# Gate and up of the second and third FFN chunk as products of scaled float16 pairs

## The chip, the cores and the metric

The kernel runs on one NeuronCore of a Trainium2 chip. The metric is the device time of one execution in microseconds (us). Besides TensorE (PE, its weight loads are listed apart as PEld) the core has VectorE (DVE), ScalarE (ACT), GpSimd (POOL) and SyncE (SP, which here only issues DMAs); each works through its own queue in order, and semaphores tie them together.

## What is computed

One step of a hybrid diffusion backbone with one layer: 128 context tokens and 1024 latent tokens, model width 1024, all in float32. Attention and a bidirectional mLSTM stand side by side behind one input projection and are merged by one output projection; the SwiGLU feed-forward network (FFN) follows. The part that matters here is its first product:

```python
def swiglu(h, w_gu, w_down):
    g, u = jnp.split(h @ w_gu, 2, axis=-1)
    return (jax.nn.silu(g) * u) @ w_down

h2 = rmsnorm(x, norm2_w) * (1 + sc2) + sh2          # sc2, sh2 from the conditioning vector
x = x + g2 * swiglu(h2, w_gu, w_down)
```

`w_gu` is 1024 x 5632 (gate and up, 2816 columns each), `w_down` 2816 x 1024. The result is wanted at about float32 accuracy. A single pass of TensorE does not hold that many bits, so the kernel splits each operand into a high and a low part and adds three products: high by high, high by low, low by high.

## The kernel before

The 1152 tokens are nine blocks of 128 (block 0 is the context), and for the FFN three chunks of three blocks (`CB = 3`, `CT = 384` tokens, `NCH = 3`). The program runs in stages: modulation and norm of the input; input projection of the keys, values and gates; four mLSTM heads, each projected while the scan of the head before is worked on beside it (`weave`, `beside`); the query projection; then, for each chunk, attention, output projection and FFN. Attention of chunk c+1 is woven into the FFN of chunk c, so from chunk 0 on TensorE always has FFN products beside the attention.

The order inside a stage is written out with Python generators: `weave(main, side, ...)` takes a step of `side` every so many units of `main`. A scheduler then orders each engine's queue by a simulated timeline of its own (`schedule_with_timeline_sim`), with some parts marked more urgent (`hot`). So a change of one instruction may shift the order of others behind it.

Weights come in pieces of 128 x 1024 float32 (512 KB). `load_piece` (L139) handles one: SP issues the DMA into a `raw` tile (two buffers), ACT casts it to the high part `whi` (L152, five buffers), and DVE (each third piece) or POOL (the others) subtracts to get the low part `wlo` (L135, five buffers). A `raw` buffer is free for the next DMA when the subtraction is done; `whi` and `wlo` are free when TensorE has used them. High and low parts are `float32r`: 4 bytes, which TensorE takes in one pass.

`norm2` (L1141) makes the FFN's input for one block: ACT scales by the row's inverse RMS, TensorE transposes, DVE (or ACT) applies the modulation, ACT casts to the high part and DVE or POOL subtracts. The two tiles `aTh` and `aTl` (`a_tiles`, L970) lie in the buffers `b2` and `b3` and serve all three chunks one after the other. `gate_up` (L1193) goes over 22 column blocks f of 128; for each it loads a gate piece and an up piece and calls `products` (L1187), 8 x 3 matmuls of 128 x 128 by 384 columns each, into one PSUM bank. The first two f of chunk 0 go through `gate_up_pair` with 256 tokens first and 128 later. Behind each f, ACT takes tanh(g/2) from PSUM, DVE forms (tanh + 1) * u * g in two operations (L1217, L1218), and ACT and POOL split the result into `hl`, high and low. After a group of four or five f, `down` (L1225) multiplies with `w_down` in matmuls of 512 columns, in two halves of the output width, and `add_gated` adds to the residual through a temporary `t2` (three buffers).

At the end of chunk c the last `down` is woven with `norm2` of chunk c+1 (L1354). A step that the change copies stands in `k_work` (L575): a scale that is a power of two, taken from the maximum of the values by a transposition on TensorE, five small DVE operations and a matmul that spreads it over the partitions.

The functions that the change touches, with their lines:

Of the kernel before, what the change touches and what calls it, by code (L numbers as in the profile page):

```python
# [2 lines left out]

# [5 lines left out]
F32 = mybir.dt.float32  # L9
# [36 lines left out]
def hybrid_step(ctx: ExitStack, tc: tile.TileContext, I: dict, O: dict):  # L46
# [71 lines left out]

    def rsqrt(tp, ss, n, inv, cap=24, plus=EPS):

        v = tp.tile([P, cap], F32, name=nm("rv"), tag="rv", bufs=2)[:, :n]
        y = tp.tile([P, cap], F32, name=nm("ry"), tag="ry", bufs=2)[:, :n]
        t = tp.tile([P, cap], F32, name=nm("rt"), tag="rt", bufs=2)[:, :n]
        h = tp.tile([P, cap], I32, name=nm("rh"), tag="rh", bufs=2)[:, :n]
        dve.tensor_scalar(out=v, in0=ss, scalar1=inv, scalar2=plus, op0=ALU.mult, op1=ALU.add)
        dve.tensor_scalar(out=h, in0=v.bitcast(I32), scalar1=1, scalar2=None, op0=ALU.logical_shift_right)
        dve.tensor_scalar(out=y.bitcast(I32), in0=h, scalar1=-1, scalar2=0x5F3759DF, op0=ALU.mult, op1=ALU.add)
        for _ in range(3):
            dve.tensor_tensor(out=t, in0=y, in1=y, op=ALU.mult)
            dve.scalar_tensor_tensor(out=t, in0=t, scalar=-0.5, in1=v, op0=ALU.mult, op1=ALU.mult)  # L130
            dve.scalar_tensor_tensor(out=y, in0=t, scalar=1.5, in1=y, op0=ALU.add, op1=ALU.mult)
        return y
# [5 lines left out]

    def load_piece(srcs, shape, dve_every=3, raw=None, own=None):  # L139

        a, b = shape
        n = a * b

        def view(t):
            return t[:, :n].rearrange("p (a b) -> p a b", b=b)

        raw = raw or wp.tile([P, 1024], F32, name=nm("raw"), tag="raw", bufs=2)
        hi = own[0] if own else wp.tile([P, 1024], F32R, name=nm("whi"), tag="whi", bufs=5)
        lo = own[1] if own else wp.tile([P, 1024], F32R, name=nm("wlo"), tag="wlo", bufs=5)
        for part, ap_ in srcs:  # L150
            dma(part(view(raw)), ap_)
        nc.scalar.copy(hi[:, :n], raw[:, :n])  # L152
# [11 lines left out]
    sil = cp.tile([P, KD, 2], F32, name="sil")  # L164
    bcol = cp.tile([P, 48], F32, name="bcol")
    ncol = cp.tile([P, 16], F32, name="ncol")
    vsc = cp.tile([P, 4], F32, name="vsc")

    es_a = ExitStack()
# [375 lines left out]
    def norm_rope(qp, cc, ss, x, nb, nh, w, rb):  # L545
# [5 lines left out]
        act(sq, xf, AF.Square)  # L551
        ssum = qp.tile([P, 20], F32, name=nm("nrs"), tag="nrs", bufs=2)[:, :n]
        dve.tensor_reduce(out=ssum, in_=sq, axis=AX.X, op=ALU.add)
# [20 lines left out]

    def k_work(qp, cc, ss, kw):  # L575
        norm_rope(qp, cc, ss, kall[:, 9:10], 1, NKV, kw, (0, 0))
# [5 lines left out]
        dma(O["new_cache_v"][0, 0], vall[:, 9])  # L582
        qone = qp.tile([1, P], F32, name="qone")
        dve.memset(qone, 1.0)

# [194 lines left out]
    def beside(*sides):  # L780

        due = [0.0] * len(sides)
        while True:
# [5 lines left out]
            yield  # L789

    es_r = ExitStack()
    ada = ada_rest(es_r.enter_context(tc.tile_pool(name="adp", bufs=1, side="right", reuse_waits="tile")))
# [33 lines left out]

    cc, ss = tables(kw)
    kwork = k_work(qp, cc, ss, kw)
# [3 lines left out]
    emit(kwork)  # L832
    scan = head_mlstm(3, sts[3])
    cc, ss = tables(qw)
# [132 lines left out]
    ft = ctx.enter_context(tc.tile_pool(name="ft", bufs=1, side="right", reuse_waits="tile"))  # L967
    fp = ctx.enter_context(tc.tile_pool(name="fp", bufs=1, side="right", reuse_waits="tile"))

    def a_tiles():  # L970
# [170 lines left out]
    def norm2(c, a, i):  # L1141

        x1 = a["x1"][i]
        if "h2" not in a:
            a["h2"] = a_tiles()
        th, tl = a["h2"]
# [3 lines left out]
        for half in range(2):  # L1150
            with hot(800):
                y = fp.tile([P, 512], F32, name=nm("y"), tag="y", bufs=2)
                act(y, x1[:, half * 512 : (half + 1) * 512], AF.Copy, scale=r)
                ps = bank()
                for j in range(4):
                    transpose(ps[:, j * P : (j + 1) * P], y[:, j * P : (j + 1) * P])
                full = both[:, half * 4 : half * 4 + 4]
                for j in range(4):
                    k = half * 4 + j
                    if j == 0 and c == 0:  # L1160
                        act(full[:, j, :], ps[:, j * P : (j + 1) * P], AF.Identity, scale=scale2[:, k, cnd : cnd + 1], bias=shift2[:, k, cnd : cnd + 1])
                        continue
                    dve.tensor_scalar(  # L1163
                        out=full[:, j, :], in0=ps[:, j * P : (j + 1) * P],
                        scalar1=scale2[:, k, cnd : cnd + 1], scalar2=shift2[:, k, cnd : cnd + 1],
                        op0=ALU.mult, op1=ALU.add)
                oh = th[:, half * 4 : half * 4 + 4, i * P : (i + 1) * P]
                nc.scalar.copy(oh, full)
                sub(tl[:, half * 4 : half * 4 + 4, i * P : (i + 1) * P], full, oh.bitcast(F32), "pool" if c == 0 else "dve")
            yield True  # L1170

    def gate_up_pair(a, fs):

        a["early"] = []
        for f in fs:
# [3 lines left out]
            for j, off in enumerate((0, D_FF)):  # L1179
                src = w_gu[:, off + f * P : off + (f + 1) * P].rearrange("(k p) n -> p k n", p=P)  # L1180
                wh, wl = load_piece([(full_view, src)], (KD, P))
                ws.append((wh, wl))
# [10 lines left out]
    def gate_up(a, f0, nf):  # L1193
# [3 lines left out]
        for f in range(f0, f0 + nf):  # L1197
# [8 lines left out]
            else:  # L1206
                pg, pu = bank(), bank()
                for off, ps in ((0, pg), (D_FF, pu)):
                    src = w_gu[:, off + f * P : off + (f + 1) * P].rearrange("(k p) n -> p k n", p=P)
                    wh, wl = load_piece([(full_view, src)], (KD, P))  # L1210
                    products(ps[:, 0:CT], wh, wl, th, tl)
# [3 lines left out]
            for cs, g, u in parts:  # L1215
                act(tn[:, cs], g, AF.Tanh, scale=0.5)
                dve.scalar_tensor_tensor(out=tn[:, cs], in0=tn[:, cs], scalar=1.0, in1=u, op0=ALU.add, op1=ALU.mult)  # L1217
                dve.tensor_tensor(out=tn[:, cs], in0=tn[:, cs], in1=g, op=ALU.mult)  # L1218
            hl = hlp.tile([P, 2, CT], F32R, name=nm("hl"), tag="hl", bufs=5)
# [70 lines left out]

    cur, nxt = {}, {}
    cur["x1"], nxt["x1"] = new_x1(0), new_x1(1)
# [49 lines left out]
    for c in range(NCH):  # L1342
        if c + 1 < NCH:
# [16 lines left out]
            cur = nxt  # L1360
            nxt = cur["next"] = {}
        else:
# [59 lines left out]
```

## Time and profile before

| what | value |
|---|---|
| runs shown | 1618.33, 1618.56, 1621.84 us; median 1618.56 |
| the profiled execution: its time, its span | 1619.03 us, 1617.1 us |
| mean granted TensorE clock in it | 0.977 |
| PE, DVE, ACT, POOL busy | 1532.5, 965.3, 689.8, 618.0 us |
| first product of the FFN, end of its last | about 623 us, about 1600 us |

A matmul's listed duration is its latency; the matmuls are pipelined, and one starts long before the one ahead of it ends. The cost of a matmul in a dense stream is the distance between two starts (called pitch here), which the timeline shows. Groups list busy time, the mean of one instruction in ns, and the idle time of the engine ahead of them with what ended it. A row of stretches gives, after the bounds and the length, the busy time and the number of instructions of PE, PEld, DVE, ACT and POOL, then the granted clock, the DMA engines' busy share and GB/s.

### The profile page before, as it was taken

Reading aid. Unit: us, or ns where it says so; the run is one execution under the profiler, and the core shown is the slowest. Engines: PE = TensorE matmul, PEld = TensorE weight load, DVE = VectorE, ACT = ScalarE, POOL = GpSimd, SP = SyncE. Lnnn points to the kernel's source line nnn. Section 1 sums busy time; section 2 is a strip of 40 time slices with the busy share of each in tenths; the row PEclk is TensorE's granted clock in tenths of the full one; section 3 lists DMA queues with packets and bytes.
Section 4 is the critical chain, followed back from the end, with each engine's and each line's share of the span. In section 5 each row is a group of like instructions: output and inputs, shape, how many; then the busy total and the mean of one; then the engine's idle time right before and its main releaser. Section 6 shows DMA issues by size and latency. Waiting matters only on the chain. (4 is left out here: it accounts for less than half of the span.)

```text
span 1617.1 us, 23358 instructions
## 1 busy us (share of the span) xinstructions
PE 1532.5 (95%) x8670; PEld 1366.1 (84%) x8670; DVE 965.3 (60%) x1969; ACT 689.8 (43%) x1193; POOL 618.0 (38%) x392
## 2 busy tenths in 40 slices
PE   6899999899898968999999999999999999999996
PEld 2888888898676757998989899898898989999995
DVE  4842363957877668577663646767674474432445
ACT  3522242424534556555643344565552453333322
POOL 1511030413345324443445344444344445544443
PEclk8999999999898988999999999999999999999998
DMA  9244443303155865777773446777684445534441
GB/s 358 67 155 125 117 142 52 82 22 71 50 183 134 180 153 116 174 181 178 180 179 113 148 153 216 188 179 175 156 185 131 131 144 176 151 127 146 144 130 65
DMA packets 386311, 232.71 MB, mean 144 GB/s; under 512 B 169910, under 2 KB 346502, under 8 KB 386198
## 3 DMA queue, kind: packets, MB, share of 16 engines
q1 hardware_dynamic: 384342, 228.04, 52.5%
q10 hardware_dynamic: 1856, 3.19, 0.6%
q8 instruction: 68, 1.11, 0.3%
q14 instruction: 45, 0.37, 0.1%
HBM read 181.16 MB, written 11.69 MB: 119 GB/s over the span
## 5 line engine op out<-in xcount | busy, mean ns | idle before, releaser
L135 POOL TENSOR_TENSOR wlo<-raw,whi 128x1024 fp32r<-128x1024 f32 (+1 forms) x159 | 390.2, 2459 | 512.3 <-ACT whi L152 474.4
L152 ACT CAST whi<-raw 128x1024 fp32r<-128x1024 f32 x239 | 245.0, 1026 | 361.7 <-DMA raw<-in_w_gu_dram 112.8
L1190 PE MATMUL mm<-aTl,whi 128*128 128x384 f32 (+2 forms) x1088 | 363.6, 334 | 0.0
L1189 PE MATMUL mm<-aTh,whi 128*128 128x384 f32 (+2 forms) x1088 | 362.5, 335 | 0.8 <-DVE tn L1217 0.8
L1191 PE MATMUL mm<-aTh,wlo 128*128 128x384 f32 (+2 forms) x1088 | 363.2, 334 | 0.0
L1189 PEld LDWEIGHTS mm<-aTh,whi 128*128 128x128 f32 x1088 | 204.5, 188 | 2.2 <-DVE tn L1217 1.4
L1190 PEld LDWEIGHTS mm<-aTl,whi 128*128 128x128 f32 x1088 | 204.9, 188 | 0.7
L1191 PEld LDWEIGHTS mm<-aTh,wlo 128*128 128x128 f32 x1088 | 204.9, 188 | 0.2
L135 DVE TENSOR_TENSOR wlo<-raw,whi 128x1024 fp32r<-128x1024 f32 (+1 forms) x80 | 98.4, 1230 | 151.7 <-ACT whi L152 147.8
L1008 PE MATMUL mm<-whi,hl 128*128 128x512 f32 x372 | 146.4, 398 | 0.8 <-ACT hl L1221 0.7
L1009 PE MATMUL mm<-wlo,hl 128*128 128x512 f32 x372 | 146.9, 396 | 0.0
L1010 PE MATMUL mm<-whi,hl 128*128 128x512 f32 x372 | 144.3, 396 | 0.8 <-POOL hl L135 0.8
L399 PE MATMUL wi<-whi,hTh 128*128 128x384 f32 (+2 forms) x392 | 135.9, 347 | 5.2 <-ACT hTh L341 5.1
L925 DVE SCALAR_TENSOR_TENSOR pl<-pr,st,ph 128x1152 f16<-128x1152 f32 (+1 forms) x72 | 111.6, 1550 | 47.7 <-ACT ph L924 47.6
L401 PE MATMUL wi<-whi,hTl 128*128 128x384 f32 (+2 forms) x392 | 133.6, 343 | 1.3 <-POOL hTl L135 1.3
L400 PE MATMUL wi<-wlo,hTh 128*128 128x384 f32 (+2 forms) x392 | 133.5, 341 | 0.0
L921 ACT ACTIVATE pr<-S,st 128x1152 f32<-128x1152 f32 (+1 forms) x72 | 81.2, 1128 | 99.7 <-DVE st L920 90.6
L135 POOL TENSOR_TENSOR hl<-tn,hl 128x384 fp32r<-128x384 f32 x66 | 83.5, 1266 | 105.0 <-ACT hl L1221 104.9
L998 DVE TENSOR_TENSOR x<-x,t 128x512 f32<-128x512 f32 x102 | 116.9, 1168 | 0.8
L1217 DVE SCALAR_TENSOR_TENSOR tn<-tn,mm 128x384 f32<-128x384 f32 (+2 forms) x68 | 36.6, 539 | 134.2 <-PE mm L1191 100.4
L918 PE MATMUL S<-kst,qT 128*128 128x384 f32 (+1 forms) x400 | 88.1, 356 | 13.9 <-ACT pr L921 13.8
L920 DVE TENSOR_REDUCE st<-S 128x1 f32<-128x1152 f32 (+1 forms) x72 | 88.8, 1233 | 20.7 <-PE S L918 20.3
(323 smaller groups left out, 2714.2 us busy)
## 6 DMA issues: line engine op xcount, KB each, us to landing
raw<-in_w_gu_dram SPq DMA_DIRECT2D x132, 512.0 KB, 4.0
raw<-in_w_down_dram SPq DMA_DIRECT2D x60, 512.0 KB, 3.6
a<-in_w_ada_dram SPq DMA_DIRECT2D x32, 512.0 KB, 4.2
gl<-g_d SPq DMA_DIRECT2D x36, 256.0 KB, 3.8
aw<-in_w_ada_dram SPq DMA_DIRECT2D x16, 512.0 KB, 8.9
raw<-in_w_in_dram SPq DMA_DIRECT2D x32, 256.0 KB, 5.6
raw<-in_w_out_dram SPq DMA_DIRECT2D x15, 512.0 KB, 4.9
x<-in_x_sample_dram SPq DMA_DIRECT2D x13, 512.0 KB, 6.4
```

The costliest lines, as they stand in the source:

```text
L135: (dve if eng == "dve" else pool).tensor_tensor(out=out, in0=full, in1=hi, op=ALU.subtract)
L152: nc.scalar.copy(hi[:, :n], raw[:, :n])
L399: mm(ps[:, :n], ah, wh[:, k % 2, c0 : c0 + n], start=(k == 0), stop=False)
L400: mm(ps[:, :n], ah, wl[:, k % 2, c0 : c0 + n], start=False, stop=False)
L401: mm(ps[:, :n], al, wh[:, k % 2, c0 : c0 + n], start=False, stop=(k == KD - 1))
L998: eng.tensor_tensor(out=x1[:, cs], in0=x1[:, cs], in1=t, op=ALU.add)
L1008: mm(ps, ah, wh[:, k % 2, :], start=(k == 0), stop=False)
L1009: mm(ps, ah, wl[:, k % 2, :], start=False, stop=False)
L1010: mm(ps, al, wh[:, k % 2, :], start=False, stop=(k == nk - 1))
L1189: mm(ps, wh[:, k, :], th[:, k, :], start=(k == 0), stop=False)
L1190: mm(ps, wh[:, k, :], tl[:, k, :], start=False, stop=False)
L1191: mm(ps, wl[:, k, :], th[:, k, :], start=False, stop=(k == KD - 1))
```

## The change

Chunk 0 computes gate and up as before. Chunks 1 and 2 hold both operands as pairs of float16 (high and low), scaled by powers of two so that they lie in float16's range, and the scale is taken out again behind the product.

- **Scale of the activations.** `norm_scale` bounds |h2| of the latent tokens by sqrt(1024) * max|scale2| + max|shift2| and makes a power of two from it with `power_scale` (a transposition, five DVE operations, a matmul, a copy). It runs as a further step behind `k_work`, in the stage of the last mLSTM heads. `sc2` and `sh2` are the modulation times that scale; `norm2` uses them from chunk 1 on, so the scaling itself adds no instruction there.
- **Scale of the weights.** While chunk 0 works on a gate or up piece, ACT runs one more pass over the `raw` tile: absolute value with a row sum (`row_sums`), 44 in all. Its output goes into a scrap tile out of the `t2` buffers. At the end of chunk 0, ahead of the last `down`, `gu_scales` takes the maximum of the sums, makes the power of two and the factors that undo both scales.
- **Pieces of chunks 1 and 2.** `load_piece(..., scale=...)` loads the float32 piece into a buffer of the `wlo` tag and keeps the float16 pair, high and low in one tile, in a buffer of the `whi` tag. Each third piece: ACT scales and casts to the high part, DVE scales and subtracts in one operation. The others: ACT scales in place, ACT casts, POOL subtracts; so ACT makes two passes where it made one. The two `raw` buffers are left to `w_out` and `w_down`.
- **Tiles.** `h2` of a chunk is one tile of 2 x 8 x 384 float16, as large as one of the two before: chunk 1 has it in `b2`, chunk 2 in `b3`.
- **Behind the product.** The tanh takes its factor from a column instead of a constant, and the second DVE operation also multiplies by a column.
- Small tiles are cut (`rsqrt`'s from 24 to 16 columns) or share a buffer (`gmx` takes that of `bcol`) to make room.

The number of matmuls of gate and up and their shapes stay. A float16 matmul stands in the program as a weight load and a matmul, where the float32r one is a single instruction that loads its weights itself.

```diff
-    def load_piece(srcs, shape, dve_every=3, raw=None, own=None):
+    def load_piece(srcs, shape, dve_every=3, raw=None, own=None, bound=None, scale=None):
...
+        if scale:
+            raw = wp.tile([P, 1024], F32, name=nm("wraw"), tag="wlo", bufs=5)
+            pair = wp.tile([P, 2, 1024], F16, name=nm("wpair"), tag="whi", bufs=5)
+            hi, lo = pair[:, 0], pair[:, 1]
...
+        lo_count[0] += 1
+        if scale:
+            if lo_count[0] % dve_every == 0:
+                act(hi[:, :n], raw[:, :n], AF.Copy, scale=scale)
+                dve.scalar_tensor_tensor(out=lo[:, :n], in0=raw[:, :n], scalar=scale, in1=hi[:, :n], op0=ALU.mult, op1=ALU.subtract)
+            else:
+                act(raw[:, :n], raw[:, :n], AF.Copy, scale=scale)
+                nc.scalar.copy(hi[:, :n], raw[:, :n])
+                sub(lo[:, :n], raw[:, :n], hi[:, :n], "pool")
+            return view(hi), view(lo)
         nc.scalar.copy(hi[:, :n], raw[:, :n])
-        lo_count[0] += 1
         sub(lo[:, :n], raw[:, :n], hi[:, :n].bitcast(F32), "dve" if lo_count[0] % dve_every == 0 else "pool")
+        if bound is not None:
+            bound(raw[:, :n])
         return view(hi), view(lo)
...
+    def power_scale(tp, one, bound, out):
+
+        ps = bank()
+        transpose(ps[0:1, 0:P], bound)
+        v = tp.tile([1, 4], F32, name=nm("pv"), tag="pv")
+        dve.tensor_reduce(out=v[:, 0:1], in_=ps[0:1, 0:P], axis=AX.X, op=ALU.max)
...
+        yield
+        ps = bank()
+        mm(ps[:, 0:2], one, v[:, 2:4], start=True, stop=True)
+        dve.tensor_copy(out, ps[:, 0:2])
+        yield
...
+    gscale = norm_scale(qp, qone)
     scan = head_mlstm(2, sts[2])
-    weave(head_project(3, sts[3]), beside((scan, 1.15), (kwork, 0.5)), 56, 56)
+    weave(head_project(3, sts[3]), beside((scan, 1.15), (chain(kwork, gscale), 0.5)), 56, 56)
...
+    sc2, sh2 = (fp.tile([P, KD], F32, name=n) for n in ("sc2", "sh2"))
+    for t, m in ((sc2, scale2), (sh2, shift2)):
+        dve.tensor_scalar(out=t, in0=m[:, :, 1], scalar1=gsc[:, 0:1], scalar2=None, op0=ALU.mult)
...
+    def row_sums(t):
+
+        def go(raw):
+            jk = ft.tile([P, D], BF16, name=nm("jk"), tag="t2", bufs=3)
+            act(jk, raw, AF.Abs, accum_out=gmx[:, t : t + 1])
+        return go
+
+    def gu_piece(a, f, off):
+
+        src = w_gu[:, off + f * P : off + (f + 1) * P].rearrange("(k p) n -> p k n", p=P)
+        if a["f16"]:
+            return load_piece([(full_view, src)], (KD, P), scale=gsc[:, 2:3])
+        return load_piece([(full_view, src)], (KD, P), bound=row_sums(f + NF * (off > 0)))
+
+    def gu_scales():
+
+        gmax = fp.tile([P, 1], F32, name="gmax")
...
+        dve.tensor_reduce(out=gmax, in_=gmx[:, 0 : 2 * NF], axis=AX.X, op=ALU.max)
+        yield from power_scale(fp, one1, gmax, gsc[:, 2:4])
+        dve.tensor_tensor(out=gsc[:, 4:5], in0=gsc[:, 1:2], in1=gsc[:, 3:4], op=ALU.mult)
...
+    def h2_tiles(c):
+        if c == 0:
+            return a_tiles()
+        t = hp.tile([P, 2, KD, CT], F16, name=nm("h2"), tag=f"b{1 + c}")
+        return t[:, 0], t[:, 1]
...
-                act(tn[:, cs], g, AF.Tanh, scale=0.5)
+                act(tn[:, cs], g, AF.Tanh, scale=gsc[:, 5:6] if a["f16"] else 0.5)
                 dve.scalar_tensor_tensor(out=tn[:, cs], in0=tn[:, cs], scalar=1.0, in1=u, op0=ALU.add, op1=ALU.mult)
-                dve.tensor_tensor(out=tn[:, cs], in0=tn[:, cs], in1=g, op=ALU.mult)
+                if a["f16"]:
+                    dve.scalar_tensor_tensor(out=tn[:, cs], in0=tn[:, cs], scalar=gsc[:, 4:5], in1=g, op0=ALU.mult, op1=ALU.mult)
+                else:
+                    dve.tensor_tensor(out=tn[:, cs], in0=tn[:, cs], in1=g, op=ALU.mult)
...
-    cur, nxt = {}, {}
+    cur, nxt = {"f16": False}, {"f16": True}
...
+            scales = gu_scales() if c == 0 else iter(())
+            next(scales, None)
-            weave(chain(down(c, cur, f0, nf, 0), down(c, cur, f0, nf, 1)), n2, 6 * nf, 8)
+            weave(chain(down(c, cur, f0, nf, 0), down(c, cur, f0, nf, 1)), chain(islice(n2, 1), scales, n2), 6 * nf, 9)
```

More of the change, by code (lines that the diff above doesn't have):

```diff
@@ L2 @@
 from contextlib import ExitStack
+from itertools import islice
 import concourse.bass as bass
@@ L573, in norm_rope, with k_work @@
         dve.tensor_tensor(out=x[:, skip:], in0=x[:, skip:], in1=t2[:, skip:], op=ALU.add)
-    def k_work(qp, cc, ss, kw):
+    def k_work(qp, cc, ss, kw, qone):
         norm_rope(qp, cc, ss, kall[:, 9:10], 1, NKV, kw, (0, 0))
@@ L827, in hybrid_step @@
     cc, ss = tables(kw)
-    kwork = k_work(qp, cc, ss, kw)
+    qone = qp.tile([1, P], F32, name="qone")
+    dve.memset(qone, 1.0)
+    kwork = k_work(qp, cc, ss, kw, qone)
+    gscale = norm_scale(qp, qone)
     scan = head_mlstm(2, sts[2])
-    weave(head_project(3, sts[3]), beside((scan, 1.15), (kwork, 0.5)), 56, 56)
+    weave(head_project(3, sts[3]), beside((scan, 1.15), (chain(kwork, gscale), 0.5)), 56, 56)
     emit(scan)
     emit(kwork)
+    emit(gscale)
     scan = head_mlstm(3, sts[3])
@@ L1159, in norm2 @@
                     k = half * 4 + j
+                    s, t = (x[:, k, cnd : cnd + 1] for x in (scale2, shift2)) if c == 0 else (x[:, k : k + 1] for x in (sc2, sh2))
                     if j == 0 and c == 0:
-                        act(full[:, j, :], ps[:, j * P : (j + 1) * P], AF.Identity, scale=scale2[:, k, cnd : cnd + 1], bias=shift2[:, k, cnd : cnd + 1])
+                        act(full[:, j, :], ps[:, j * P : (j + 1) * P], AF.Identity, scale=s, bias=t)
                         continue
[L1163 to L1166, printed above, removed]
+                    dve.tensor_scalar(out=full[:, j, :], in0=ps[:, j * P : (j + 1) * P], scalar1=s, scalar2=t,
+                                      op0=ALU.mult, op1=ALU.add)
                 oh = th[:, half * 4 : half * 4 + 4, i * P : (i + 1) * P]
                 nc.scalar.copy(oh, full)
-                sub(tl[:, half * 4 : half * 4 + 4, i * P : (i + 1) * P], full, oh.bitcast(F32), "pool" if c == 0 else "dve")
+                sub(tl[:, half * 4 : half * 4 + 4, i * P : (i + 1) * P], full, oh.bitcast(F32) if c == 0 else oh,
+                    "pool" if c == 0 else "dve")
             yield True
@@ L1360, in hybrid_step @@
             cur = nxt
-            nxt = cur["next"] = {}
+            nxt = cur["next"] = {"f16": True}
         else:
```

40 lines of the change are left out of this document (27 added, 13 removed).

## The prediction

> **What bounds the kernel now.** I read the page's table of engines and its slices first, then busy times by stretch, then single matmuls in the timeline, last the waits of ACT and of SP's queue.
>
> ```profile
> PE 1532.5 (95%) x8670; PEld 1366.1 (84%) x8670; DVE 965.3 (60%) x1969; ACT 689.8 (43%) x1193; POOL 618.0 (38%) x392
> PE   6899999899898968999999999999999999999996
> PEclk8999999999898988999999999999999999999998
> ```
>
> From the sixteenth slice on PE is full at full clock. The stretches of the FFN say it sharper (chunk 0 with attention woven in, its rest, the same of chunk 1, chunk 2):
>
> ```profile
> core 0: us, PE busy (x) PEld busy (x) DVE busy (x) ACT busy (x) POOL busy (x), PEclk, DMA share, GB/s
> 660.00:918.00 258.00, 257.16 (x1424) 234.97 (x1424) 158.68 (x209) 123.04 (x161) 107.87 (x53) 1.00 0.67 168
> 918.00:1004.00 86.00, 85.71 (x475) 81.14 (x474) 50.24 (x93) 37.97 (x55) 40.33 (x21) 1.00 0.56 172
> 1004.00:1260.00 256.00, 252.47 (x1406) 228.09 (x1405) 173.18 (x231) 131.88 (x172) 106.60 (x49) 1.00 0.68 169
> 1260.00:1327.00 67.00, 66.90 (x357) 61.60 (x356) 37.01 (x65) 32.48 (x46) 31.97 (x17) 1.00 0.45 138
> 1327.00:1597.00 270.00, 269.24 (x1428) 252.35 (x1427) 110.86 (x145) 89.14 (x117) 131.51 (x66) 1.00 0.46 140
> ```
>
> PE idles 5.5 us in these 937; ACT is busy 33 to 52% of a stretch, POOL 42 to 49%. So the pitch of the matmuls is the time here, and ACT and POOL have room. Pitches, at clock 1.00, from first and last row of dense streams:
>
> ```profile
> 913.55 0.34 PE L1191 MATMUL mm<-aTh,wlo 128*128 128x384 f32 x1
> 923.43 0.34 PE L1191 MATMUL mm<-aTh,wlo 128*128 128x384 f32 x1
> ...
> 630.16 0.28 PE L1191 MATMUL mm<-aTh,wlo 128*128 128x256 f32 x1
> 633.46 0.28 PE L1189 MATMUL mm<-aTh,whi 128*128 128x256 f32 x1
> ...
> 1188.83 0.27 PE L942 MATMUL po<-phT,vs 128*128 128x256 f16 x1
> 1189.92 0.27 PE L942 MATMUL po<-phT,vs 128*128 128x256 f16 x1
> ```
>
> 57 steps in 9.88 us: 173.3 ns for 384 float32r columns. 28 steps in 3.30 us: 117.9 ns for 256. 10 steps in 1.09 us: 109.0 ns for 256 float16 columns, each matmul with a weight load of its own. At equal width float16 is 8.9 ns ahead.
>
> **The change part by part.**
>
> *Products.* How many move, and what their weight loads cost:
>
> ```profile
> L1191 PE MATMUL mm<-aTh,wlo 128*128 128x384 f32 x1024 | 344.9, 337 | 0.0
> L1191 PEld LDWEIGHTS mm<-aTh,wlo 128*128 128x128 f32 x1088 | 204.9, 188 | 0.2
> L942 PEld LDWEIGHTS <-vs 128*128 128x128 f16 x292 | 29.1, 100 | 26.0 <-issue 9.5 <-DVE oT L947 6.1 <-DMA phT<-ph 5.9
> ```
>
> Three lines of 1024 are 3072 matmuls of 384 columns; chunk 0 has 40 pieces at that width (960), chunks 1 and 2 have 44 each: 88 x 24 = 2112. No float16 matmul of 384 columns is in the trace. If its pitch goes with the columns it is 109.0 x 1.5 = 163.5 ns, 9.8 less; if the advantage is a fixed 8.9 ns, 164.4. That is 20.7 or 18.8 us; I take 20, as both come from the same nearby row. The separate weight load (100 against 188 ns) lies under the stream of 164. The other bound is no gain at all (rival B). The Trainium skill, "TensorE: Matmul & The Clock Gate", section Back-to-back issue gap, has N/2.4 + 2.5 ns for the warm array; for 256 columns that is 109.2, as the trace shows for float16, and for 384 it is 162.5, by which the gain would be an estimated 22.8 us.
>
> *Row sums.* 44 passes on ACT in chunk 0, like the norm's square sum, and in chunks 1 and 2 a second pass for two pieces of three:
>
> ```profile
> L1137 ACT ACTIVATE jk<-x 128x1024 bf16<-128x1024 f32 x15 | 15.8, 1052 | 9.7 <-DVE x L998 7.1 <-POOL x L998 2.6
> L1137 ACT ACTIVATION_READ_ACCUMULATOR jk<-x 128x1 f32 x15 | 2.8, 188 | 0.0
> L152 ACT CAST whi<-raw 128x1024 fp32r<-128x1024 f32 x227 | 237.6, 1048 | 334.0 <-DMA raw<-in_w_gu_dram 112.8 <-PE mm L1190 56.1 <-DMA raw<-in_w_down_dram 49.3
> L135 POOL TENSOR_TENSOR wlo<-raw,whi 128x1024 fp32r<-128x1024 f32 x153 | 382.6, 2504 | 500.6 <-ACT whi L152 462.7 <-issue 14.7 <-DVE t L997 12.9
> raw<-in_w_gu_dram SPq DMA_DIRECT2D x132, 512.0 KB, 4.0
> 660.00:918.00 258.00, 85.19 (x252) 47.44 (x252) 1.00 0.67 168
> 660.00:918.00 258.00, 40.40 (x102) 19.25 (x102) 1.00 0.67 168
> ```
>
> (The last two rows are L1189 and L1008 alone, in the woven stretch of chunk 0.) 44 x 1.24 = 55 us of ACT. In that stretch 252/8 = 31.5 gate and up pieces and 102/6 = 17 of `down` pass: ACT goes from 123 to 162 of 258 us, 63%. The path is the `raw` buffer: 4.0 us landing, 1.05 cast, 2.5 subtraction (7.6), two buffers, so one piece in 3.8 us, while PE takes one in 258/48.5 = 5.3 there and one in 24 x 0.1733 = 4.16 within a gate/up run. The sum runs on ACT while POOL subtracts, so it lengthens a buffer's turn only when ACT is late. Queued behind it on ACT are the next cast, tanh and, in the woven part, the attention's exponentials; behind the DMA that waits for the buffer, on SP, the attention's transposing DMAs. `t2`, the scrap tile, also ties the sum to DVE's `add_gated`. Bounds 0 and 30 us (rival A); I take 1.5, near the end of no cost, because of these waits:
>
> ```profile
> ACT whi L152 <- PE mm L1190: 63.9, 34, 4.2
> ACT whi L152 <- PE mm L1010: 58.8, 23, 4.7
> PE mm L1189 <- DVE tn L1217: 0.8, 2, 0.5
> SPq L151 <- POOL wlo L135: 348.0, 118, 39.3
> ```
>
> ACT waits for PE to give back a `whi` buffer (123 us), not PE for ACT: the pieces run ahead of PE.
>
> *Pieces in float16.* Two thirds of 88 pieces, 59 x 1.05 = 62 us more on ACT: chunk 1's woven stretch goes from 132 to about 160 of 256, chunk 2 from 89 to about 120 of 270. Nothing on the path: the float32 pieces now turn in five buffers instead of two, which pays for the longer chain (4.0 + 1.05 + 1.05 + 2.5 = 8.6 us against 5 x 3.92 of PE). POOL's subtraction into float16 and DVE's fused one:
>
> ```profile
> L135 POOL TENSOR_TENSOR vs<-vall,vs 128x640 f16<-128x640 f32 x2 | 2.9, 1467 | 5.8 <-DVE vs L874 5.8
> L925 DVE SCALAR_TENSOR_TENSOR pl<-pr,st,ph 128x1152 f16<-128x1152 f32 x64 | 105.3, 1645 | 47.1 <-ACT ph L924 47.0
> L135 DVE TENSOR_TENSOR wlo<-raw,whi 128x1024 fp32r<-128x1024 f32 x74 | 94.3, 1274 | 127.1 <-ACT whi L152 123.3 <-DMA a<-in_w_ada_dram 3.5
> ```
>
> 2.3 ns per element on POOL is no dearer than 2504/1024; DVE goes from 1.27 to 1.46 us for 29 pieces, 6 us in a queue 41 to 68% busy. Bounds 0 and 5 us together; I take 0.5. The operations behind the product keep their count and size.
>
> *Scale of the activations.* Nine DVE operations on a column or less, two tiny matmuls, in the stage of the last heads, where PE waits for its transposition. A copy of `k_work`'s step. At worst each matmul waits for a run of small DVE operations:
>
> ```profile
> L923 DVE TENSOR_SCALAR st<-st 128x1 f32<-128x1 f32 x72 | 10.9, 152 | 1.9
> L131 DVE SCALAR_TENSOR_TENSOR ry<-rt,ry 128x1 f32<-128x1 f32 x27 | 7.4, 273 | 0.5
> ```
>
> 5 x 0.15 to 0.27, twice, at most 3 us; other heads' matmuls stand between, so 0.5. From this step on the scheduler orders all queues anew up to the FFN, with an unknown of 4 us to both sides and no mean.
>
> *Scale of the weights.* In the changed program's order the transposition of the maximum stands behind chunk 0's last gate/up product, the matmul that spreads the scale 40 products of `down` later, and 52 more products of 512 columns and 20 transpositions stand ahead of chunk 1's first float16 product. The third float32 piece may load only when DVE is through with the first. From the scale on: DVE copy, scaled cast 1.05, DVE 1.46, DMA 4.0, two ACT passes 2.1, and ACT's last cast of `h2` behind them, about 9.5 us with 2 of queueing 11.5; PE has 52 x 0.232 (0.39 us latency, pitch from the timeline below) + 20 x 0.11 = 14.3. Covered by 3 us; if ACT or DVE is later than that, PE stands.
>
> ```profile
> 1594.14 0.39 PE L1275 MATMUL mm<-wlo,hl 128*128 128x512 f32 x1
> 1594.61 0.39 PE L1275 MATMUL mm<-wlo,hl 128*128 128x512 f32 x1
> 1000.00:1050.00 50.00, 47.12 (x252) 42.32 (x251) 31.84 (x42) 26.78 (x33) 23.07 (x10) 1.00 0.76 211
> ```
>
> (Two steps in 0.47 us.) Before, PE already idles 2.9 us around this border. Bounds -2 and +8; I take +1.5.
>
> *Sum.* -20 + 1.5 + 0.5 + 0.5 + 1.5 = -16 against the profiled execution's 1619.0: 1603. Its median sibling is 1618.56, 0.5 lower; within what a measurement can tell, about 0.2% or 3.2 us. I say 1602.5.
>
> **The rivals.**
>
> *A, slower: chunk 0 becomes bound by its pieces.* If the sum and one exponential with its accumulator read (1.4 us at most) fall into each buffer's turn, it is 7.6 + 1.24 + 1.4 = 10.2 us, 5.1 per piece against 4.16 in a gate/up run. Over 32 pieces of the woven part that is 30 us: 1619 - 16 + 28.5 = 1631. It beats the gain from a turn of 8.3 + 2 x 16/32 = 9.3 us on. For it: DMAs wait 348 us for POOL to give a buffer back. Against: ACT at 63%, PE's own demand of 5.3 us per piece there, and pieces ahead of PE. A mild form (half) ends at 1616.
>
> *B, float16 is no faster at this width.* If at 384 columns something other than the operand's width sets 173 ns (the accumulation, the column count), the gain is zero and the additions of 4 us stay: 1623. For it: only 256 columns are shown. Against: float32r exceeds it at that width, and 173.3 and 117.9 lie on the same line of 0.45 ns a column. The Trainium skill, same page, section on weight-path perf modes, says that "the array processes one element per cell per cycle regardless of element width"; by that a one-pass float32r matmul would gain nothing from two bytes and the time would be 1623. The trace's 109.0 against 117.9 at 256 columns disagrees with that for float32r.
>
> *C, the scale is late at the border.* Each microsecond beyond the 3 us of cover is one of PE idle; with 8 us: 1609.
>
> **How the numbers follow.** Forecast (1595 to 1609) 0.67, C 0.08, A mild 0.07, A full 0.06, B 0.07, a worse order ahead of the FFN 0.05 (1610 to 1622). The range 1594 to 1618 leaves out full A, B and a part of the last. Faster: forecast, C, half of mild A and of the last: 0.80; same (1615.3 to 1621.8) 0.07, slower 0.13.
>
> **What would show it.** The L1269 to L1271 products (new numbering) 163 to 165 ns apart in chunks 1 and 2, weight loads near 100 ns; chunk 2 shorter by 10 us; chunk 0 as long as before with PE idle under 2 us; ACT about 63% in chunk 0. Wrong if PE waits in chunk 0 for `whi`, `wlo` or a DMA, if PE stands over 5 us at the border to chunk 1, or if the pitch stays at 173.

## The result and the profile after

The change made the kernel slower: 1643.72 us (median of four runs, 1643.06 to 1647.05) against 1618.44, a ratio of 1.015 with a 95% interval of 1.0133 to 1.0167. That is 25.3 us more where 16 less were forecast, outside the stated range.

The engines and slices of the page, after:

```profile
PE 1526.9 (93%) x8676; PEld 1218.4 (74%) x8676; DVE 960.8 (59%) x1991; ACT 796.3 (48%) x1337; POOL 598.9 (36%) x392
PE   6899999899878877999999999998999999999996
PEclk9999999999888987999999999999999999999998
```

The stretches from one chunk's first gate/up product to the next one's (ahead of the FFN from 465 us on; chunk 0; chunk 1; chunk 2 to the end). Columns are those of the prediction's stretches. Before:

```profile
465.00:622.60 157.60, 126.95 (x617) 101.21 (x615) 116.99 (x220) 83.92 (x128) 59.14 (x35) 0.88 0.69 163
622.60:976.70 354.10, 352.54 (x2024) 324.02 (x2022) 218.69 (x319) 172.82 (x232) 154.76 (x78) 1.00 0.64 161
976.70:1327.60 350.90, 346.98 (x1923) 316.83 (x1921) 229.43 (x330) 175.96 (x234) 150.65 (x71) 1.00 0.64 167
1327.60:1617.10 289.50, 275.94 (x1455) 257.45 (x1453) 125.76 (x195) 94.89 (x131) 134.76 (x69) 0.98 0.44 135
```

After:

```profile
465.00:631.20 166.20, 131.45 (x637) 106.08 (x636) 121.33 (x227) 84.74 (x132) 68.22 (x39) 0.87 0.67 153
631.20:1001.70 370.50, 357.73 (x2007) 326.35 (x2007) 202.97 (x325) 219.00 (x320) 147.78 (x74) 0.99 0.64 158
1001.70:1360.30 358.60, 342.53 (x1920) 240.61 (x1919) 232.93 (x333) 205.79 (x262) 138.39 (x70) 0.98 0.66 162
1360.30:1642.20 281.90, 265.94 (x1453) 177.48 (x1452) 128.00 (x194) 125.96 (x157) 125.94 (x69) 0.98 0.48 138
```

The lengths tell where the time went: 8.6 us ahead of the FFN, 16.4 in chunk 0, 7.7 in chunk 1, and 7.6 back in chunk 2. The gain is there: PE's busy time falls by 4 us in chunk 1 and by 10 in chunk 2. But its idle time grows from 1.6 to 12.8 us in chunk 0 and from 3.9 to 16.1 in chunk 1, while ACT rises from 49 and 50 to 59 and 57% of them.

The stalls cost more than their own length. The granted clock is 1.00 through chunks 0 and 1 before; after the change, five stretches in them run at 0.50: 643.5 to 650.3 and 940.5 to 943.9 us in chunk 0, 1005.3 to 1012.1, 1145.3 to 1148.7 and 1216.9 to 1220.3 in chunk 1. Each begins less than 4 us after PE stopped for 1.5 us or more. One of them, with the stretch before it and the one behind it:

```profile
936.00:940.50 4.50, 0.68 (x3) 0.35 (x3) 1.11 (x2) 3.56 (x6) 2.44 (x2) 1.00 0.44 122
940.50:943.90 3.40, 3.40 (x11) 3.40 (x12) 0.00 (x0) 0.94 (x2) 3.22 (x2) 0.50 0.56 156
943.90:947.00 3.10, 3.10 (x19) 3.10 (x18) 0.00 (x0) 0.56 (x1) 0.00 (x0) 1.00 0.60 169
```

PE does 11 products in 3.4 us and then 19 in 3.1. At half clock stand 10.2 us of chunk 0 and 13.6 of chunk 1, about 5.1 and 6.8 us of work lost. With that chunk 1 comes out: 12.2 us more idle and 6.8 lost, less 1056 products at 10.9 ns (11.5), come to an estimated 7.5 of the measured 7.7.

Single products of the changed kernel in dense streams, float16 in chunk 2 and float32r in chunk 0:

```profile
1436.11 0.33 PE L1270 MATMUL mm<-h,wpair 128*128 128x384 f16 x1
1439.52 0.33 PE L1270 MATMUL mm<-h,wpair 128*128 128x384 f16 x1
...
946.50 0.34 PE L1269 MATMUL mm<-aTh,whi 128*128 128x384 f32 x1
951.80 0.34 PE L1269 MATMUL mm<-aTh,whi 128*128 128x384 f32 x1
```

Float16: 21 steps in 3.41 us, 162.4 ns. Float32r: 30 steps in 5.30 us, 176.7 ns where 173.3 stood before, for products that the change did not touch.

What SP's queue waits for in chunk 0, after (line, releaser, us in total, times, longest):

```profile
SPq L157 <- POOL wlo L136: 66.1, 39, 3.6
SPq L157 <- ACT jk L1024: 47.8, 22, 5.3
SPq L157 <- DVE wlo L136: 31.7, 16, 4.6
```

The same before:

```profile
SPq L151 <- POOL wlo L135: 77.2, 31, 4.7
SPq L151 <- DVE wlo L135: 42.1, 16, 8.3
```

So 22 loads of chunk 0 have a wait for a row sum. Matched piece by piece, though, 34 of the 44 sums end before the piece's own subtraction and hold nothing. The other ten, the first two pieces of each of the five groups of f, end 6 to 49 us after it; before, the loads that reuse these buffers went out within 0.8 us of the subtraction. One such pair (the subtractions of the two pieces end at 693.3 and 700.5 us):

```profile
691.00 1.05 ACT L168 CAST whi<-raw 128x1024 fp32r<-128x1024 f32 x1 [3.63 <-DMA raw<-in_w_gu_dram]
696.96 1.05 ACT L168 CAST whi<-raw 128x1024 fp32r<-128x1024 f32 x1 [1.87 <-PE mm L1091]
705.56 0.58 ACT L941 CAST qT<-mm 64x512 fp32r<-64x512 f32 x1 [7.56 <-PE mm L115]
707.50 1.06 ACT L1024 ACTIVATE jk<-raw 128x1024 bf16<-128x1024 f32 x1
708.67 0.38 SPq L157 DMA_DIRECT2D raw<-in_w_gu_dram  x1
```

ACT is not busy there. It stands 7.56 us in front of a copy for the attention that waits for PE, and the sums are queued behind that copy; the next load goes out when the first sum is done. PE in chunk 0 and, below the dots, in chunk 1:

```profile
PE mm L1269 <- ACT whi L168: 7.4, 3, 3.6
...
PE S L963 <- ACT pr L966: 9.3, 6, 3.4
PE mm L1269 <- DVE t L1078: 2.2, 1, 2.2
```

and in chunk 1 before:

```profile
PE S L918 <- ACT pr L921: 1.7, 1, 1.7
```

In chunk 0 PE stands for weight pieces: its two stretches at half clock follow on the first and the last of the five groups. In chunk 1 it stands most of all for the attention's exponentials (`pr`).

### The profile page after: what moved, and what is told of

The parts are those of the page before. It is cut to its first block, busy times and chain, and to the rows that moved or that the text cites. A ratio compares the mean times of both kernels' runs of the same rounds, so it can differ in the third digit from the quotient of the medians.

```text
span 1642.2 us, 23495 instructions
## 1 busy us (share of the span) xinstructions
PE 1526.9 (93%) x8676; PEld 1218.4 (74%) x8676; DVE 960.8 (59%) x1991; ACT 796.3 (48%) x1337; POOL 598.9 (36%) x392
## 5 line engine op out<-in xcount | busy, mean ns | idle before, releaser
L136 POOL TENSOR_TENSOR wlo<-raw,whi 128x1024 fp32r<-128x1024 f32 x103 | 245.8, 2389 | 368.9 <-ACT whi L168 359.0
L168 ACT CAST whi<-raw 128x1024 fp32r<-128x1024 f32 (+1 forms) x151 | 152.6, 1011 | 190.6 <-DMA raw<-in_w_gu_dram 47.6
L1270 PE MATMUL mm<-h,wpair 128*128 128x384 f16 x704 | 231.9, 330 | 4.3 <-DVE h L136 4.3
L1269 PE MATMUL mm<-h,wpair 128*128 128x384 f16 x704 | 231.1, 329 | 2.9 <-DVE t L1078 2.7
L1271 PE MATMUL mm<-h,wpair 128*128 128x384 f16 x704 | 231.5, 330 | 0.0
L136 POOL TENSOR_TENSOR wpair<-wraw,wpair 128x1024 f16<-128x1024 f32 x56 | 124.6, 2233 | 213.9 <-ACT wpair L165 211.3
L1090 PE MATMUL mm<-wlo,hl 128*128 128x512 f32 x372 | 147.2, 396 | 0.0
L1269 PE MATMUL mm<-aTh,whi 128*128 128x384 f32 (+2 forms) x384 | 127.5, 333 | 7.4 <-ACT whi L168 7.4
L1270 PE MATMUL mm<-aTl,whi 128*128 128x384 f32 (+2 forms) x384 | 127.7, 333 | 0.0
L1271 PE MATMUL mm<-aTh,wlo 128*128 128x384 f32 (+2 forms) x384 | 127.6, 333 | 0.0
L136 DVE TENSOR_TENSOR wlo<-raw,whi 128x1024 fp32r<-128x1024 f32 (+1 forms) x48 | 55.8, 1162 | 95.3 <-ACT whi L168 91.5
L1079 DVE TENSOR_TENSOR x<-x,t 128x512 f32<-128x512 f32 x102 | 107.3, 1065 | 1.0
L1271 PEld LDWEIGHTS <-wpair 128*128 128x128 f16 x704 | 69.6, 99 | 50.3 <-issue 7.1
```

The costliest lines, as they stand in the source:

```text
L136: (dve if eng == "dve" else pool).tensor_tensor(out=out, in0=full, in1=hi, op=ALU.subtract)
L1079: eng.tensor_tensor(out=x1[:, cs], in0=x1[:, cs], in1=t, op=ALU.add)
L1090: mm(ps, ah, wl[:, k % 2, :], start=False, stop=False)
L1269: mm(ps, wh[:, k, :], th[:, k, :], start=(k == 0), stop=False)
L1270: mm(ps, wh[:, k, :], tl[:, k, :], start=False, stop=False)
L1271: mm(ps, wl[:, k, :], th[:, k, :], start=False, stop=(k == KD - 1))
```

## The experiments

Medians in us, each difference against the kernel before in the same job, its ratio with the 95% interval, and the lengths of the same four stretches in the profiled execution (the first one from 0). The profiled execution of e1 took 1646.3 us, 6 more than its median:

| run | median, difference | ratio | to chunk 0 | chunk 0 | chunk 1 | chunk 2 to end |
|---|---|---|---|---|---|---|
| before | 1618.4 | | 622.6 | 354.1 | 350.9 | 289.5 |
| the change | 1643.7, +25.3 | 1.015 [1.0133, 1.0167] | 631.2 | 370.5 | 358.6 | 281.9 |
| e1 | 1640.2, +21.9 | 1.0139 [1.0113, 1.0166] | 639.2 | 369.9 | 355.2 | 280.2 |
| e2 | 1626.8, +8.5 | 1.005 [1.0034, 1.0066] | 621.5 | 357.6 | 354.0 | 292.1 |
| e3 | 1613.7, -4.6 | 0.9967 [0.9956, 0.9979] | 623.2 | 353.5 | 353.4 | 280.0 |
| e4 | 1631.3, +13.0 | 1.0078 [1.0062, 1.0094] | 620.6 | 367.5 | 350.5 | 289.7 |
| e5 | 1631.3, +11.2 | 1.0068 [1.0049, 1.0086] | 622.4 | 373.0 | 353.1 | 278.1 |
| e6 | 1622.9, +2.7 | 1.0017 [1.0005, 1.0029] | 618.2 | 357.3 | 350.8 | 289.7 |
| e7 | 1610.6, -9.5 | 0.9945 [0.9928, 0.9962] | 625.6 | 355.1 | 349.1 | 278.7 |
| e8 | 1584.8, -35.3 | 0.9784 [0.9764, 0.9803] | 620.2 | 339.3 | 340.1 | 280.2 |
| e9 | 1600.8, -17.4 | 0.99 [0.988, 0.9921] | 624.5 | 353.7 | 344.3 | 280.6 |
| e10 | 1634.5, +16.4 | 1.0104 [1.0089, 1.0119] | 623.2 | 354.0 | 361.2 | 294.4 |
| e11 | 1639.3, +21.1 | 1.0147 [1.0121, 1.0174] | 630.8 | 369.8 | 354.3 | 278.3 |
| e12 | 1641.9, +23.8 | 1.0152 [1.0137, 1.0168] | 634.8 | 373.1 | 354.4 | 277.9 |
| e13 | 1630.0, +11.8 | 1.0082 [1.0061, 1.0104] | 634.9 | 357.7 | 352.5 | 278.3 |
| e14 | 1615.4, -2.9 | 0.9978 [0.9962, 0.9994] | 637.0 | 360.0 | 338.3 | 276.2 |
| e15 | 1576.3, -41.9 | 0.9737 [0.9719, 0.9755] | 621.2 | 333.7 | 341.7 | 274.2 |

### The place of the buffers (e1, e2)

In the built program the new tile `gsc` (24 bytes a partition, 32 as it is placed) lies ahead of the weight buffers; `whi`, `wlo` and `raw` begin at multiples of 64 bytes before, and 32 beyond one after. `aTh` and `aTl` lie at the same addresses in the kernel before, the change, e1 and e2, so of a gate or up product's operands only the weights moved.

```diff
-    gsc = cp.tile([P, 6], F32, name="gsc")
+    gsc = cp.tile([P, 16], F32, name="gsc")        # e1: the change, all else as it is
...
     vsc = cp.tile([P, 4], F32, name="vsc")
+    pad = cp.tile([P, 8], F32, name="pad")         # e2: the kernel before, all else as it is
```

> The changed kernel with its scale tile gsc widened from 6 to 16 columns, 24 to 64 bytes a partition; order and operations of all queues unchanged. gsc lies ahead of the pool of weight buffers and moved every raw, whi and wlo from a multiple of 64 bytes to 32 beyond one; the wider tile moves them back to a multiple of 64. Theory P (place): the float32r products of chunk 0, which stand 176 to 178 ns apart after the change and stood 173 apart before, are slower because of the buffers' place; they return to 173, which is 960 x 3.5 = 3.4 us, about 2 us more come back in `down`, and the time is 1636 to 1640. Theory Q (the queues, ACT above all): place is nothing, 1643 to 1645, pitch still 177.

> The kernel before with one unused tile of 32 bytes ahead of the weight buffers; order and operations of all queues unchanged. Theory P: 3072 products at 3.5 ns more are 10.7 us, and `down` 2 us: 1629 to 1632, with products 176 to 178 ns apart. Theory Q: 1618 to 1619, and 173 ns.

Dense float32r streams of e1:

```profile
958.03 0.34 PE L1269 MATMUL mm<-aTh,whi 128*128 128x384 f32 x1
963.75 0.34 PE L1269 MATMUL mm<-aTh,whi 128*128 128x384 f32 x1
```

and of e2:

```profile
930.07 0.34 PE L1190 MATMUL mm<-aTh,whi 128*128 128x384 f32 x1
939.61 0.34 PE L1190 MATMUL mm<-aTh,whi 128*128 128x384 f32 x1
```

33 steps in 5.72 us are 173.3 ns; 54 in 9.54 are 176.7. Each queue holds the same instructions in the same order in both pairs, so the place of the weights does this: 8.5 us where all products are float32r, about 3.4 in the change (its float16 products keep 162 ns in either place). Theory P holds for the pitch; e2 stayed 2 us under its forecast, since not every product slowed by the full 3.5 ns (over the whole run the median is 176 ns, and a quarter stands at 174 or less).

### Row sums (e4, e6, e13)

```diff
+        if bound is not None:
+            bound(raw[:, :n])                       # e4: Abs with row sum, on the kernel before
-            bound(raw[:, :n])
+            bound(hi[:, :n].bitcast(F32))           # e6: e4 with this; e13: e1 with this
```

> The kernel before with the 44 row sums on ACT in chunk 0 and nothing else: all pieces float32r, buffers at multiples of 64 bytes. Theory Q: the sums hold ACT and the raw buffers, PE stands in chunk 0 as after the change, some 10 to 15 us: 1629 to 1634. Theory P: the sums are hidden, 1619 to 1621.

> The row sums alone on the kernel before, but taken of whi (five buffers) in place of raw (two buffers): ACT does the same 44 passes, and a raw buffer is free as soon as cast and subtraction have read it. Theory B (the sum holds the raw buffer, and the next DMA with it): most of the 13 us go, 1619 to 1623. Theory A (ACT's time, whichever buffer it reads): 1629 to 1633.

> The run with the wide gsc, with the row sums taken of whi in place of raw; all else of the change stays. Alone on the kernel before, that move gave back some 8 to 10 of the 13 us. If the parts add up: 1630 to 1633, and the SP queue no longer waits for the sums. If in the whole change another wait takes the place (ACT, the scale at the border): 1637 to 1641.

Chunk 0 of e4 and its loads:

```profile
620.60:988.10 367.50, 357.24 (x2022) 325.52 (x2021) 201.18 (x318) 218.79 (x320) 151.11 (x78) 0.99 0.63 158
...
SPq L151 <- ACT jk L984: 36.2, 21, 6.3
```

and of e6:

```profile
618.20:975.50 357.30, 353.90 (x2024) 324.22 (x2022) 222.20 (x318) 218.51 (x320) 149.77 (x78) 1.00 0.63 160
```

ACT is as busy in both (218.8 and 218.5 us). Only in e4 do loads wait for the sum, and there chunk 0 takes 13.4 us more; in e6 it takes 3.2 more. The scrap tile out of `t2` is the same in both. So it is the buffer, not ACT's time: in e4, too, ten sums end 6 to 61 us after the subtraction, and 34 before it. Inside the whole change the same move is worth 10.1 us (21.9 - 11.8).

### Pieces in float16 (e3, e7, e9, e10)

e3 has constants for all scales. e7 drops the second pass on top of that, e9 and e10 change the buffer that the float32 piece is loaded into.

```diff
-                act(raw[:, :n], raw[:, :n], AF.Copy, scale=scale)    # e7 (from e3), e9
                 nc.scalar.copy(hi[:, :n], raw[:, :n])
...
-            raw = wp.tile([P, 1024], F32, name=nm("wraw"), tag="wlo", bufs=5)
+            raw = wp.tile([P, 1024], F32, name=nm("wraw"), tag="raw", bufs=2)   # e9 (from e7), e10 (from e3)
```

> The wide gsc, and constants for all scales: no row sums in chunk 0, no scale of the activations, no scale of the weights at the border; the float16 pieces of chunks 1 and 2 with their scaled passes stay. It leaves out how the scales are found, and its scales fit this input alone. Theory Q: ACT's row sums are what made PE stand in chunk 0 (15 us) and at the border, its second passes what made it stand in chunk 1 (18 us): chunk 0 is back to 354 us, chunk 1 stays at 355 to 360 us, chunk 2 at 268; 1612 to 1620. Theory P alone (no stall comes from ACT): 1636 to 1640 as the run with the wide gsc. A third theory, that a new order of the queues by the scheduler costs 10 us wherever it comes from: chunk 0 stays over 360 us without the row sums.

> The run with constant scales, with weights left unscaled: each float16 piece takes one cast on ACT as a float32r piece does, and the second pass is gone for two pieces of three. It leaves out the scale of the weights, so that their low halves lie in float16's smallest numbers. If ACT's second pass is what makes PE stand in chunk 1: the 22 us of idle time there fall to 5 to 9 as before the change, and the time is 1596 to 1601. If the stalls come from the order of the queues or the longer chain of buffers: 1611 to 1615.

> The run with one pass and constants, with one edit: the float16 pieces load into the two raw buffers again and no longer into the five wlo buffers, which they shared with the float32r pieces of `down` and of the output projection. In that run PE still stood 18.6 us in chunk 1 against 7.0 before the change. Theory R (ring): a load into wlo waits until PE has used up an earlier low half, so pieces come late; without it the stalls of chunk 1 fall to 5 to 9 us, 1596 to 1601. Theory S (the stalls come with the order that the scheduler finds for float16 pieces, or with the activations' conversion): 1608 to 1612.

> The run with constant scales and both passes of ACT, loading into the two raw buffers. Theory R with cheap second passes: 1598 to 1603. If the longer turn of a raw buffer (4.0 + 1.05 + 1.05 + 2.5 = 8.6 us, two buffers, so one piece in 4.3 us against PE's 3.9 in a dense run) becomes the bound instead: 0.4 us for each of some 50 pieces in dense runs, 20 us, 1615 to 1625.

e3 brings chunk 0 back to 353.5 us and leaves chunk 1 at 353.4, near what theory Q had (354, and 355 to 360). My next step was wrong: without the second pass (e7) only 5.0 us came back and not 15. The loads of e7 in chunk 1 show a wait that neither the kernel before nor e9 has, a weight load that waits for PE:

```profile
SPq L157 <- PE mm L1122: 6.5, 3, 4.5
SPq L157 <- PE mm L1089: 5.5, 1, 5.5
SPq L157 <- PE mm L1090: 5.2, 5, 2.7
```

L1088 to L1090 are `down` there and L1122 the output projection: they hold `wlo` until PE has used it, and a float16 piece's load into that ring stands in SP's queue until then, and what is queued behind it, the attention's transposing DMAs among it, waits too. With loads into `raw` (e9) chunk 1 falls by 4.8 us in the profiled executions, and the time by 7.8. e10 shows why the ring was used: with two passes on two buffers ACT waits longer for loads (143 us for gate and up pieces, 105 in e9), and chunks 1 and 2 take 31 us more than in e9, more than the 20 I had worked out (a piece in 4.3 us against 3.9). ACT from chunk 1 on in e10 and, below the dots, in e9:

```profile
ACT wraw L164 <- DMA wraw<-in_w_gu_dram: 82.7, 47, 5.7
ACT wpair L161 <- DMA wraw<-in_w_gu_dram: 60.3, 24, 5.4
...
ACT wpair L164 <- DMA wraw<-in_w_gu_dram: 60.8, 28, 5.1
ACT wpair L161 <- DMA wraw<-in_w_gu_dram: 44.5, 18, 4.5
```

### The step that scales the activations (e5, e11, e12)

```diff
-    gscale = norm_scale(qp, qone)                  # e5: e1 with two constants instead
+    for at, v in ((0, 64.0), (1, 1 / 64)):
+        dve.memset(gsc[:, at : at + 1], v)
...
-    ... (chain(kwork, gscale), 0.5) ...
+    ... (chain(gscale, kwork), 0.5) ...            # e11: e1 with this
...
     weave(linear_tok(w_q, 0, 512, ev_q, QFIRST), scan, 24, 60)
     emit(scan)
+    emit(gscale)                                   # e12: e1 with the step here
```

> The run with the wide gsc, with a constant in place of the scale of the activations alone (its scale fits this input alone): row sums and the scale of the weights stay. In that run and in the changed kernel PE falls some 9 us behind between 470 and 565 us, while the queries are projected and attention begins, where no row sum and no float16 piece exists yet; the runs without the scale of the activations do not show it. Theory O (the step's nine small operations cost nothing where they stand, but the scheduler orders the queues anew from there on, and the new order is worse): the lag is gone, 1629 to 1633. Theory W (the lag comes with the row sums or the scale of the weights, which the scheduler also sees): 1638 to 1641.

> The run with the wide gsc, with the step that scales the activations put ahead of the keys' work in place of behind it. Same operations; the scheduler's order from there on is another one. Theory O (order): PE's lag behind the kernel before at the end of the queries' projection (565 us) is another one than the 9 us of the changed kernel, anywhere from -2 to 15 us, and the total moves with it. If the step's operations themselves cost the 9 us: again 9, and 1638 to 1642.

> The run with the wide gsc, with the step that scales the activations put behind the first part of the queries' projection. Same operations, a third order. Theory O: the lag at 565 us is again another one, -2 to 15 us. If the operations themselves cost 9 us: 9 us, and 1638 to 1642.

The stretch of the queries' projection, about 100 us behind the step, in the kernel before, the change, e5, e11 and e12:

```profile
470.00:565.00 95.00, 85.04 (x413) 67.79 (x412) 70.93 (x127) 45.62 (x71) 40.46 (x24) 0.93 0.75 184
```

```profile
470.00:565.00 95.00, 78.45 (x381) 63.39 (x382) 73.16 (x133) 46.95 (x76) 33.51 (x19) 0.90 0.71 165
```

```profile
470.00:565.00 95.00, 84.14 (x414) 67.92 (x413) 71.49 (x128) 45.63 (x71) 39.82 (x24) 0.93 0.76 184
```

```profile
470.00:565.00 95.00, 73.19 (x340) 56.97 (x339) 64.59 (x121) 41.62 (x69) 32.78 (x20) 0.85 0.62 159
```

```profile
470.00:565.00 95.00, 80.44 (x378) 64.67 (x379) 69.13 (x127) 46.04 (x75) 38.06 (x23) 0.91 0.66 168
```

PE does 4.6 to 11.9 us less in this stretch with the step, by its place, and 0.9 less without. The step's first reduction runs at 291 us in the change and its spreading matmul at 361, and from 360 to 470 us PE is busy 99.4 us there and 100.4 before. In all runs without the step chunk 0 begins at 618 to 626 us, in all with it at 631 to 639. So the loss lies well behind the step, where only the order of the queues differs: up to chunk 0 PE stands once 7.0 us for `norm2`'s scaled rows and once 5.7 for the attention's `qT` in the change, and for neither in e5. With the step in its first place PE is busy 75.9 to 78.5 us of this stretch (the change, e1, e13, e14), so e11 and e12 do differ by its place, as theory O says; but their totals came out where its rival put them. How the order brings the loss is argued, not shown. And a single profile can't size it: with one order, chunk 0 begins at 631.2 us in the change and at 639.2 in e1. Taking the step away is worth 10.7 us (21.9 - 11.2). Whether a place exists where it costs nothing is open: three were tried, none did.

### One pass everywhere, and the change mended (e8, e14, e15)

e8 is the kernel before with float16 pairs, unscaled, in all three chunks; e15 has them in `down` too. e14 is e13 with both remedies for the pieces, scales found as in the change.

```diff
+        if f16:                                     # e8, e15
+            pair = wp.tile([P, 2, 1024], F16, name=nm("wpair"), tag="whi", bufs=5)
+            hi, lo = pair[:, 0], pair[:, 1]
...
-            if lo_count[0] % dve_every == 0:        # e14: ACT scales and casts, DVE scales and subtracts, for every piece
+            if True:
```

> The kernel before with float16 pairs for gate and up in all three chunks, unscaled on both sides, one cast and one subtraction a piece, raw in its two buffers: only the type differs from before. It leaves out all scales. 3072 products of 384 columns at 10.6 ns less are 32.6 us, 128 of the others 1 us: 1584 to 1590 if PE's pitch still sets the time in chunk 0; 1592 to 1600 if the pieces' chain through two raw buffers (7.6 us for two) becomes the bound in the dense runs, where PE then takes one in 3.9 us.

> The same, and the float16 pieces load into the two raw buffers and take one scaled pass on ACT, with DVE's fused subtraction for all of them in place of one in three. If the parts add up: 10 us less for the ring and 3 for the second passes, 1617 to 1621. If DVE (59 more subtractions of 1.46 us, 86 us on a queue that is 68% busy in chunk 1) becomes what PE waits for: 1625 to 1640.

> The run with float16 pairs in one pass in all chunks, and `down` in float16 pairs as well, unscaled. It leaves out all scales. 1188 products of 512 columns at 232 - 216 = 16 ns less (216 by 162.5 and 109 ns at 384 and 256 columns, 0.42 ns a column) are 19 us: 1564 to 1569 if PE's pitch sets the time; 1572 to 1582 if pieces then come late, since PE needs one in 3.9 us and the two raw buffers give one in 3.8.

e8 and e15 leave out all scales, and e3, e7, e9 and e10 take constants: what they gain holds for this input. The prices add up: e13 lands where the sum of the single runs put it, e14 2 us under. e14 is the one that finds its scales and still beats the kernel before, by 2.9 us (0.2%). Chunk 1 of e14:

```profile
997.00:1335.30 338.30, 334.91 (x1921) 238.72 (x1921) 243.52 (x361) 180.35 (x232) 75.09 (x42) 0.99 0.71 173
```

It takes 12.6 us less than before the change, with DVE 72% busy and not yet in the way. Without scales e8 is 2.2% under the kernel before, with an interval on both sides of 2%. e15 is another 0.5% under it, but 7 to 12 us over what its pitch would give. Its `down`:

```profile
1452.08 0.38 PE L1020 MATMUL mm<-wpair,hl 128*128 128x512 f16 x1
1454.02 0.38 PE L1020 MATMUL mm<-wpair,hl 128*128 128x512 f16 x1
```

9 steps in 1.94 us, 215.6 ns, as forecast. In its chunk 1

```profile
954.90:1296.60 341.70, 331.83 (x1923) 205.66 (x1921) 223.23 (x330) 175.83 (x234) 134.46 (x71) 0.99 0.69 172
```

PE idles 9.9 us; there the pitch alone no longer sets the time.

## Why the prediction was wrong

Following the prices along the runs (differences to before): e9 -17.4, ring +7.8 (e7), second pass +5.0 (e3), row sums and the scale of the weights +15.7 (e5), scale of the activations +10.7 (e1), place +3.4 (the change), together +25.3. The 95% intervals of the two runs overlap for the second pass and the place, so these two prices are loose; the other steps are clear of them.

- **Products**: right. Taken 20 us; 162.4 ns instead of 173.3 on 2112 products are 23.0. The formula of the Trainium skill, "TensorE: Matmul & The Clock Gate", section Back-to-back issue gap, was nearer than my row (162.5 ns, and 215.8 at 512 columns; the traces show 162.4 and 215.6). Rival B fell, and with it what the Trainium skill says in "TensorE: Matmul & The Clock Gate", section on weight-path perf modes, as I had read it for float32r.
- **Row sums**: the step that failed first. I took 1.5 us near the end of no cost; alone they cost 13.0. The buffer was rival A's, `raw`, and the size a little under half of its full one, but the mechanism was another: the turn did not grow for every piece. 34 of 44 sums hid behind the subtraction, as I had taken it; the first two of each group stood in ACT's in-order queue behind work that waits for PE and held both buffers 6 to 49 us. I had set this near nothing by averages: ACT at 63%, pieces ahead of PE. "Late" was not a matter of how busy ACT is.
- **Pieces in float16**: taken 0.5 us, "nothing on the path". The five `wlo` buffers that I counted as room are shared with pieces that PE holds. That ring cost 7.8, the second pass 5.0. Between e9's -17.4 and the 23.0 of pitch 5.6 more remain, most of them in chunk 1, where PE idles 8.5 us in e9 and 3.9 before, and where 3.4 us run at half clock; these were not separated.
- **Scale of the activations**: the unknown of 4 us to both sides for a new order was too small; 10.7, all of it a loss. I gave a worse order 0.05.
- **Scale of the weights**: right in size. e5 against e3 is 15.7, of which the sums are 13.0, so 2.7 where 1.5 was taken. Rival C did not happen: the spreading matmul ran at 986.5 us, 15 us ahead of chunk 1's first product. PE stood at this border all the same, 3.4 us from 1001.7 to 1006 behind DVE's residual and `h` operations, with 6.8 us at half clock behind that. Nor did it idle there before: the row with 2.9 us begins 23 us behind the border, and from 950 to 988 us PE was busy throughout.
- **Clock**: not in the prediction. Each price above holds what its stalls cost at half clock, 5.1 us of chunk 0 and 6.8 of chunk 1 in the change.
- **Place**: not in the prediction. 3.4 us from 32 bytes.

Of what was to show it, the pitch and the weight loads (99 ns) came as said, and chunk 2 was 7.6 us shorter where 10 were said; chunk 0 was to be as long as before and grew by 16.4 us, with PE waiting for `whi`, which was named as a sign of being wrong.

## What to carry to other kernels

Where the matmuls' pitch is the time, float16 pairs in place of float32r pairs pay, if the pieces keep one pass, their own load buffers and a short turn; here that is 17 us for two chunks and 35 for three without scales, and 3 us for two with scales that the program finds. An added reader of a load buffer costs what it delays the next load, however idle its engine looks on average: look at what stands ahead of it in its engine's queue, or let it read a copy that lives longer (10 us here). Where the granted clock falls behind a stall of the matmuls, the stall costs more than its length: here 24 us at half clock in chunks 0 and 1 come on top. A ring that is shared with tiles which PE holds is not spare room, and a small tile may move all buffers behind it: look where they begin.

## What the runs showed of the hardware

Moving the weight buffers by 32 bytes within SBUF slowed float32r products of 384 columns from 173.3 to 176.7 ns, with every queue unchanged; float16 products did not react. Of these products' operands only the weights moved; `aTh` and `aTl` stayed 32 bytes beyond a multiple of 64. No other step than 32 bytes was tried.

Behind stalls of PE of 1.5 to 3.6 us in chunks that ran at clock 1.00 before, the profile shows 3.4 or 6.8 us at clock 0.50, with float16 products of 384 columns about 320 ns apart where 162 stand at full clock. Not every such stall has it: one of 1.8 us at 1074 us has none.
